# Two turns of a gated linear attention leave TensorE for VectorE blocks and GpSimd transfers

## The chip, the cores and the metric

The kernel runs on one core of one Trainium2 chip. The metric is device time in microseconds (us) of one execution. The kernel before was timed three times: 907.1, 907.38 and 908.11 us, median 907.38 us.

## The reference, cut to what matters

Two layers run one after the other on 256 frames of width 2048. Each layer projects its input once, runs three groups of heads on the result (eight heads of banded softmax attention, four heads of gated linear attention, four heads of cross-attention into 256 memory tokens), gates them, projects back and normalizes. The change touches the linear attention alone:

```python
gate_logit = b_lr @ gate_w + gate_b                 # b_lr: (256, 16), gate_w: (16, 256)
log_g = jax.nn.log_sigmoid(gate_logit) / GATE_TAU
def step(state, inp):                               # one chunk of 64 frames, every head
    qc, kc, vc, gc = inp
    b = jnp.cumsum(gc, axis=1)
    decay = jnp.exp(-jnp.abs(b[:, :, None] - b[:, None, :]))
    attn = jnp.einsum('bihd,bjhd,bijhd->bhij', qc, kc, decay)
    o_intra = jnp.einsum('bhij,bjhv->bihv', attn, vc)
    o_inter = jnp.einsum('bihd,bhdv->bihv', qc * jnp.exp(b), state)
    k_dec = kc * jnp.exp(b[:, -1][:, None] - b)     # decayed keys
    new_state = jnp.exp(b[:, -1])[..., None] * state + jnp.einsum('bjhd,bjhv->bhdv', k_dec, vc)
    return new_state, o_intra + o_inter
```

Two operands stand the wrong way round for TensorE, which sums over partitions. `b_lr` comes out of its projection with frames on partitions, and its product with `gate_w` sums over the 16 gate inputs. `k_dec` is made with features on partitions, and its product with `vc` sums over frames.

## The kernel before, in words

All large projections have one form. A weight piece is loaded by SyncE's queue (SP) into `raw`; ScalarE (ACT) rounds it into a high part `wh` (L124), VectorE (DVE) subtracts to make the low part `wl` (L125), and TensorE multiplies the parts with high and low parts `x` of the input into `acc`. Three products stand for one product in full precision. The pools hold four buffers each of `raw`, `wh` and `wl`, so a cast into `wh` waits until TensorE has finished the piece four before it. A piece is 388 or 512 columns wide.

The order of TensorE's and SP's instructions is that of the program text. Heads are Python generators: after every weight piece of the big projections a clock called `tick` moves on (by 1 for 512 columns, by 0.76 for 388) and the generators that are due put their matrix products between two pieces. A `yield 6` in a generator means that its next products stand at least six ticks later in TensorE's order. Two generators are in turn at a time, three once the linear attention is done. The order on DVE, ACT and GpSimd (POOL) is chosen by the build's scheduler from its own estimate of when things are ready; on the chip each engine then keeps that order, and an instruction that waits holds up everything behind it on its engine.

`gla` is the generator of the linear attention, once per layer. Its steps in the kernel before:

- `lr` holds the 16 gate inputs with frames on partitions, three times side by side (high, low, high; columns 48 to 127 are zero). TensorE turns it with two transposes against an identity (L366), DVE copies the result to `lrT` (L368). `yield 2`.
- Two products of `gw` and `lrT` give the gate's logits (first product at L372, issued through L102), ACT adds the bias (L375), and the chain L378 (DVE), L379 and L380 (ACT, Exp and Ln, each with a table of its own), L381 and L386 (DVE, the last one the cumulative sum `b_`) follows.
- The decayed keys `kd`: a subtraction (L390, DVE), an Exp (L392, ACT) and the product with the keys (L393, DVE). `qe`, `eb` and `elast` are made beside it. `yield 6`.
- TensorE turns `kd` with four transposes (L419) into a PSUM bank; ACT copies it to `kdT` (L421). `yield 2`.
- Twelve small products of `kdT` with the values (`kv` banks), 32 products of undecayed keys and queries, and 32 products of the first level of `decayed` (L404 to L412: subtraction on DVE, Abs and Exp on ACT, two products `kl` and `ql` on DVE). They all stand in one block in TensorE's order. The further levels and the output follow later.

In the trace, scratch tiles, `kd` and `kdT` among them, all carry the name `sc`, and all PSUM banks the name `bk`.

Another way of turning is used elsewhere in the same kernel: `turned` (L549 to L559). DVE turns every 32x32 block of a tile in place of the block (L554), POOL issues one transfer of the tile to a DRAM buffer `home` (L556), waits for its landing, and issues four transfers back, each to 32 partitions, with the blocks in their new places (L559).

Of the kernel before, what the change touches and what calls it, by code (L numbers as in the profile page):

```python
# [8 lines left out]
F32 = mybir.dt.float32  # L9
F32R = mybir.dt.float32r  # L10
# [8 lines left out]
P = 128  # L19
D = 2048  # L20
T = 256
# [15 lines left out]
def hybrid_trunk_kernel(  # L37
# [7 lines left out]
    pe, dve, act, pool, sp = nc.tensor, nc.vector, nc.scalar, nc.gpsimd, nc.sync  # L45
# [30 lines left out]
    def finish(gens):  # L76
        while not all(g in done for g in gens):
            tick()

    def enter(name, bufs=1, **kw):  # L80
        return ctx.enter_context(tc.tile_pool(name=name, bufs=bufs, **kw))
# [5 lines left out]
    hd = enter("hd", 1)  # L87
    tp = enter("tp", 3)
    sc = enter("sc", 8)
    sm = enter("sm", 1)  # L90
    psd = enter("psd", 2, space=bass.MemoryType.PSUM)
    psa = enter("psa", 4, space=bass.MemoryType.PSUM)
    drm = enter("drm", 6, space=bass.MemoryType.DRAM)
# [3 lines left out]
    def nm(s):  # L97
        uid[0] += 1
        return f"{s}_{uid[0]}"

    def mm(o, l, r, start, stop):
        pe.matmul(o, l, r, start=start, stop=stop, skip_group_check=True)  # L102

    def bank():
        return psa.tile([P, 512], F32, name=nm("bk"), tag="bk")

    def scratch(shape, dtype=F32):
        return sc.tile(shape, dtype, name=nm("sc"), tag="sc")
# [4 lines left out]
    ident = cst.tile([P, P], F32, name="ident")  # L113
# [180 lines left out]
    def as_group(src, xq, n, kp=2, first=None, need={}):  # L294

        acc = psd.tile([P, 2, 512], F32, name=nm("acc"), tag="acc")
        for pc in range(16 // kp):
            if first is not None and pc % 2 == 0:
                xq.append(load_quarter(first[pc // 2]))
            finish(need.get(pc, ()))  # L300
            w = piece(src[pc], n, kp)
            for kk in range(kp):
                for t in range(2):
                    as_products(acc[:, t, :n], t, xq, w, pc * kp + kk, kk)
            tick(n / 512)
        return acc
# [12 lines left out]
    def gla_inputs(l):  # L319

        gw = sm.tile([P, 256], F32R, name=nm("gw"), tag="gw")
        raw = hd.tile([48, 256], F32, name=nm("gwraw"), tag="pairs0")
        gb = small([P, 2], "gb")
        ng = small([P, 1], "ng")
        for i in range(3):
            sp.dma_start(raw[i * 16:i * 16 + 16], gate_w[l])
        pool.memset(gw.bitcast(F32), 0.0)
        tc.keep_in_program_order(act.copy(gw[:48], raw))
        tc.keep_in_program_order(dve.tensor_tensor(gw[32:48], raw[32:], gw[32:48].bitcast(F32), op=ALU.subtract))
        sp.dma_start(gb, gate_b[l])  # L330
        sp.dma_start(ng, norm_g[l])
        return gw, gb, ng

    def gla(gw, gb, ng, gq, gk, lr, asv, yraw):
        gqf = gq.rearrange("p b t -> p (b t)")
        gkf = gk.rearrange("p b t -> p (b t)")
        pairs = [hd.tile([P, 4, CH], F32, name=nm("pairs"), tag=f"pairs{par}") for par in range(2)]
# [23 lines left out]
                    dve.copy_predicated(pairs[par], lmask[:, lev].unsqueeze(1).to_broadcast([P, 4, CH]), pv)  # L361


        pt = bank()
        for t in range(2):
            pe.transpose(pt[:, t * P:(t + 1) * P], lr[:, t].bitcast(F32), ident)  # L366
        lrT = sm.tile([P, T], F32R, name=nm("lrT"), tag="lrT")
        dve.tensor_copy(lrT, pt[:, :T])  # L368
        yield 2
        pl = bank()  # L370
        for b in range(2):
            mm(pl[:, b * T:(b + 1) * T], gw[:, b * P:(b + 1) * P], lrT, True, True)  # L372
        xx = scratch([P, 512])
        for b in range(2):
            act.activation(xx[:, b * T:(b + 1) * T], pl[:, b * T:(b + 1) * T], AF.Identity, bias=gb[:, b:b + 1])  # L375
# [13 lines left out]
        kd = scratch([P, 512])  # L389
        dve.tensor_tensor(kd.rearrange("p (g c) -> p g c", c=CH),  # L390
                          bc[:, :, CH - 1:CH].to_broadcast([P, 8, CH]), bc, op=ALU.subtract)
        act.activation(kd, kd, AF.Exp, scale=1.0 / 16)  # L392
        dve.tensor_tensor(kd, gkf, kd, op=ALU.mult)  # L393
        eb = scratch([P, 512])
        act.activation(eb, b_, AF.Exp, scale=1.0 / 16)
        elast = small([P, 8], "elast")
# [16 lines left out]
            return kl, ql  # L413


        pt = bank()
        for t in range(2):
            for b in range(2):
                pe.transpose(pt[:, (t * 2 + b) * P:(t * 2 + b + 1) * P], kd[:, b * T + t * P:b * T + t * P + P], ident)  # L419
        kdT = scratch([P, 4, P])  # L420
        act.copy(kdT, pt.rearrange("p (g c) -> p g c", c=P))  # L421
        yield 2
        nxt = [decayed(LEVELS[0])]
        kv = [bank() for _ in range(2)]
        for c in range(3):
            rs = slice((c % 2) * 64, (c % 2) * 64 + 64)
            t = c // 2
            for b in range(2):
                for par in range(2):
                    h = 2 * b + par  # L430
                    mm(kv[c % 2][par * 64:par * 64 + 64, (t * 2 + b) * P:(t * 2 + b + 1) * P],
                       kdT[rs, t * 2 + b, par * 64:par * 64 + 64],
                       asv[rs, t, 16 + h * P:16 + (h + 1) * P], True, True)

        low, high = bank(), bank()
# [3 lines left out]
        st = hd.tile([P, 3, 2, P], F32, name=nm("st"), tag="st")  # L439
        for c in range(3):  # L440
            t = c // 2
# [29 lines left out]
        for t in range(2):  # L471
            for b in range(2):
                g = t * 2 + b
# [5 lines left out]
        for odd, even in ((1, 2), (3, None)):  # L479
            for b in range(2):  # L480
                for c in (odd, even):
                    if c is not None:
                        for par in range(2):
                            g = (c // 2) * 2 + b
# [64 lines left out]
    def turned(n, *todo):  # L549

        homes = []
        for _, src in todo:
            blocks = scratch([P, 4, n])
            dve.transpose(blocks.rearrange("p b (g j) -> p g b j", j=32), src.rearrange("p (g b j) -> p g b j", b=4, j=32))  # L554
            homes.append(drm.tile([P, 4, n], F32, name=nm("home"), tag=f"home{n}"))
            pool.dma_start(homes[-1], blocks)  # L556
        for (dst, _), home in zip(todo, homes):
            for b in range(4):
                pool.dma_start(dst[b * 32:(b + 1) * 32], home[:, b].rearrange("(a i) n -> i a n", a=4))  # L559
# [72 lines left out]
    def transposed(xq, gbT):  # L632

        raw, gT = gbT
        pt = bank()
        pe.transpose(pt[:, :P], raw, ident)
        dve.tensor_copy(gT, pt[:, :32])
        for q in range(4):
            x = operand()
            hi, lo, _ = x  # L640
            xq.append(x)
            for j in range(0, 4, 2):
                pt = bank()
                y = scratch([P, 2, T])
                for jj in range(2):
                    kt = q * 4 + j + jj
                    for t in range(2):
                        pe.transpose(pt[:, jj * T + t * P:jj * T + (t + 1) * P], res[:, t, kt * P:(kt + 1) * P], ident)  # L648
                with tc.high_priority(AHEAD // 4):
                    for jj in range(2):  # L650
                        kt = q * 4 + j + jj
                        src, g, b = pt[:, jj * T:(jj + 1) * T], gT[:, kt:kt + 1], gT[:, 16 + kt:17 + kt]
                        if jj == 0:
                            act.activation(y[:, jj], src, AF.Identity, bias=b, scale=g)
                        else:
                            dve.tensor_scalar(y[:, jj], src, g, b, op0=ALU.mult, op1=ALU.add)
                    parts(hi[:, j:j + 2], lo[:, j:j + 2], y)
                yield 1

    def restored(gb):  # L660

        for n in range(WO_N):
            for t in range(2):
                r = res[:, t, columns(n)]
                tc.keep_in_program_order(dve.tensor_tensor(r, r, gb[n][0], op=ALU.mult))
                dve.tensor_tensor(r, r, gb[n][1], op=ALU.add)
                yield 2
# [150 lines left out]
    for l in range(L):  # L818
# [20 lines left out]
        else:  # L839
            memq = []  # L840
            parts(*mv, as_group(w512[l, G_MV], memq, 512, 2, memT))
            gens = [transposed(xq, gbT), restored(gb)]
# [5 lines left out]
        gq = hd.tile([P, 2, T], F32, name=nm("gq"), tag="gq")  # L848
        gk = hd.tile([P, 2, T], F32, name=nm("gk"), tag="gk")
# [9 lines left out]
        gp = gla_inputs(l)  # L859
# [6 lines left out]
        asv = per.tile([P, 2, 1552], F32, name=nm("asv"), tag="asv")  # L866

        def values(i):
            acc = as_group(w388[l, i], xq, 388)
            act.copy(asv[:, :, i * 388:(i + 1) * 388], acc[:, :, :388])  # L870
# [9 lines left out]
        lr = hd.tile([P, 2, P], F32R, name=nm("lr"), tag="qe")  # L880
        pool.memset(lr.bitcast(F32), 0.0)
        values(0)
        for i in (0, 32):
            act.copy(lr[:, :, i:i + 16], asv[:, :, :16])
        dve.tensor_tensor(lr[:, :, 16:32], asv[:, :, :16], lr[:, :, :16].bitcast(F32), op=ALU.subtract)
        values(1)
        if l == 0:
            sp.dma_start(res, xn.rearrange("(t p) d -> p t d", p=P))
# [9 lines left out]
            finish(gens)  # L898
        yraw = [per.tile([P, 4, T], F32, name=nm("yr"), tag=f"yr{i}") for i in range(4)]
        finish(early_gens)  # L900
        gens = [[gla(*gp, gq, gk, lr, asv, yraw[0])]]
        waiting.extend(gens[0])
        linear[:] = gens[0]
        for half in range(2):
# [35 lines left out]
        gb = []  # L940
# [148 lines left out]
```

## Time and profile before

| what | value |
|---|---|
| median of three runs | 907.38 us |
| profiled execution, its own time | 907.3 us |
| its span (first to last instruction) | 905.5 us |
| granted TensorE clock, mean | 0.999 |
| TensorE busy (matmul row) | 898.8 us |
| DVE, ACT, POOL busy | 605.4, 480.3, 176.0 us |
| bytes moved by DMA | 207.16 MB |

The views used below are the page's busy line and its chain of work that ended last, the waits of one engine, and the timeline (start and length in us, engine, line, operation, written tile<-read tiles, partitions x elements, count, and in brackets the idle time of the engine just before and what ended it). Times of the timeline count from the span's start. In the timeline, matmuls overlap each other, so what one costs is read from the distance between the starts of its neighbours, not from its own length.

### The profile page before, as it was taken

How to read it: one execution, taken by the hardware profiler on the slowest of the kernel's cores; microseconds unless marked ns; L12 is line 12 of the kernel's file. 1: busy time of each engine (PE TensorE's matmuls, PEld its weight loads, DVE VectorE, ACT ScalarE, POOL GpSimd, SP SyncE). 2: the span in 40 equal slices, each digit the busy share in tenths (PEclk: the TensorE clock that was granted, in tenths of full speed). 3: DMA queues.
4: the chain of work that ended last, by engine and by line, in shares of the span. 5: the costliest groups of instructions: out<-in, count | busy, mean ns of one | idle time of the engine just before them, and what ended most of it. 6: DMA issues, size and time to landing. Idle time of an engine off the chain costs nothing.

```text
span 905.5 us, 13967 instructions
## 1 busy us (share of the span) xinstructions
PE 898.8 (99%) x4926; PEld 773.8 (85%) x4926; DVE 605.4 (67%) x878; ACT 480.3 (53%) x695; POOL 176.0 (19%) x329
## 2 busy tenths in 40 slices
PE   9999999999999999999999999999999999999997
PEld 8889998998888888888888899889888888888885
DVE  6765478757566676565587676885756586766766
ACT  6654475474544656433466445754745365744440
POOL 0002002015043543200000220021141433334000
PEclk9999999999999999999999999999999999999999
DMA  9977876668787988776775686666696879889752
GB/s 313 319 214 216 299 219 194 182 205 268 216 245 206 275 260 274 225 263 188 232 250 168 202 245 204 198 194 202 192 287 195 261 209 277 253 232 280 232 164 93
DMA packets 131512, 207.16 MB, mean 229 GB/s; under 512 B 14313, under 2 KB 99689, under 8 KB 131185
## 3 DMA queue, kind: packets, MB, share of 16 engines
q1 hardware_dynamic: 117744, 173.28, 61.3%
q0 software_dynamic: 13408, 32.59, 13.1%
q8 instruction: 38, 0.62, 0.3%
q10 hardware_dynamic: 288, 0.39, 0.1%
q14 instruction: 34, 0.27, 0.1%
HBM read 189.93 MB, written 16.25 MB: 228 GB/s over the span
## 4 chain that ended last, share of the span: by engine, by line
PE 99%; DMA 0%; DVE 0%; ACT 0%; issue 0%
PE acc L102 90%; PE bk L102 8%; PE bk L648 0%; DMA raw<-w 0%; PE bk L419 0%; ACT res L804 0%; DVE stats L789 0%; PE bk L366 0%; DVE res L788 0%; ACT wh L124 0%; DVE res L740 0%; DVE mvt L743 0%; PE bk L792 0%; ACT nparts L124 0%; DVE rs_u L751 0%
## 5 line engine op out<-in xcount | busy, mean ns | idle before, releaser
L102 PE MATMUL acc<-wh,x 128*128 128x512 f32 (+2 forms) x2196 | 656.2, 380 | 0.2 <-ACT wh L124 0.2
L125 DVE TENSOR_TENSOR wl<-raw,wh 128x1024 fp32r<-128x1024 f32 (+3 forms) x321 | 368.0, 1151 | 190.2 <-ACT wh L124 188.5
L124 ACT CAST wh<-raw 128x1024 fp32r<-128x1024 f32 (+3 forms) x321 | 318.8, 995 | 320.2 <-PE acc L102 256.4
L102 PEld LDWEIGHTS acc<-wh,x 128*128 128x128 f32 x2196 | 405.5, 188 | 63.4 <-ACT wh L124 0.5
L102 PE MATMUL acc<-wl,x 128*128 128x512 f32 (+2 forms) x1098 | 414.7, 378 | 0.0
L102 PEld LDWEIGHTS acc<-wl,x 128*128 128x128 f32 x1098 | 205.9, 188 | 34.0 <-DVE wl L125 0.4
L556 POOL DMA_DIRECT2D home<-sc x58 | 32.5, 561 | 494.3 <-DVE sc L554 483.9
L102 PE MATMUL acc<-x,wh 128*128 128x512 f32 x288 | 91.1, 398 | 0.0
L102 PEld LDWEIGHTS acc<-x,wl 128*128 128x128 f32 x288 | 54.1, 188 | 12.6
L559 POOL DMA_DIRECT2D pT<-home x96 | 52.6, 554 | 41.4 <-DMA home<-sc 26.7
L102 PE MATMUL acc<-x,wl 128*128 128x256 f32 x288 | 56.7, 278 | 0.0
L102 PEld LDWEIGHTS acc<-x,wh 128*128 128x128 f32 x288 | 44.8, 189 | 1.3 <-ACT wh L124 0.2
L559 POOL DMA_DIRECT2D zT<-home x48 | 26.2, 553 | 32.8 <-DMA home<-sc 17.6
L559 POOL DMA_DIRECT2D yr<-home x48 | 26.1, 551 | 16.2 <-DMA home<-sc 7.9
L554 DVE STREAM_TRANSPOSE sc<-sc 128x512 f32<-128x512 f32 (+1 forms) x36 | 22.6, 642 | 1.9 <-ACT sc L931 1.4
L578 ACT ACTIVATE sc<-sc,mx 128x128 f32<-128x128 f32 (+1 forms) x32 | 14.4, 449 | 17.2 <-DVE mx L576 17.2
L538 DVE TENSOR_TENSOR sc<-zT,yr 128x256 f32<-128x256 f32 x24 | 8.9, 415 | 21.3 <-DMA zT<-home 21.3
L408 ACT ACTIVATE sc<-sc 128x512 f32<-128x512 f32 x12 | 7.6, 633 | 14.9 <-DVE sc L406 14.9
L124 ACT CAST x<-sc 128x512 fp32r<-128x512 f32 x20 | 11.8, 617 | 7.0 <-DVE sc L538 5.7
L571 DVE SCALAR_TENSOR_TENSOR sc<-bk,bias 128x384 f32<-128x384 f32 x16 | 8.7, 543 | 9.5 <-PE bk L102 9.5
L554 DVE STREAM_TRANSPOSE sc<-acc 128x512 f32<-128x512 f32 x18 | 11.8, 693 | 3.6 <-PE acc L102 2.8
L559 POOL DMA_DIRECT2D qk<-home x24 | 13.1, 553 | 5.0 <-DMA home<-sc 5.0
(211 smaller groups left out, 587.5 us busy)
## 6 DMA issues: line engine op xcount, KB each, us to landing
raw<-w SPq DMA_DIRECT2D x323, 256.0 KB, 4.2
raw<-w SPq DMA_DIRECT2D x94, 512.0 KB, 4.9
raw<-w SPq DMA_DIRECT2D x64, 388.0 KB, 3.5
home<-sc POOLq DMA_DIRECT2D x42, 256.0 KB, 4.4
bias<-relw SPq DMA_DIRECT2D x16, 192.0 KB, 4.6
yr<-home POOLq DMA_DIRECT2D x48, 64.0 KB, 4.7
home<-sc POOLq DMA_DIRECT2D x16, 192.0 KB, 3.2
pT<-home POOLq DMA_DIRECT2D x64, 48.0 KB, 4.2
```

The lines of the kernel that those rows point to most:

```text
L102: pe.matmul(o, l, r, start=start, stop=stop, skip_group_check=True)
L124: act.copy(hi, src)
L125: dve.tensor_tensor(lo, src, hi.bitcast(F32), op=ALU.subtract)
L408: act.activation(dd, dd, AF.Abs)
L538: dve.tensor_tensor(o, z, r, op=ALU.mult)
L554: dve.transpose(blocks.rearrange("p b (g j) -> p g b j", j=32), src.rearrange("p (g b j) -> p g b j", b=4, j=32))
L556: pool.dma_start(homes[-1], blocks)
L559: pool.dma_start(dst[b * 32:(b + 1) * 32], home[:, b].rearrange("(a i) n -> i a n", a=4))
L571: dve.scalar_tensor_tensor(s, pb[:, :384], SCALE, bias[h], op0=ALU.mult, op1=ALU.add)
L578: act.activation(s[:, own[t]], s[:, own[t]], AF.Exp, bias=mx[:, t:t + 1], accum_out=zs[:, t:t + 1])
```

## The change

Both turns of the linear attention use DVE and POOL. For `lr`, DVE turns 32x32 blocks of its first 64 columns right after `lr` is made, POOL writes them to a DRAM buffer and reads them back with two transfers into a 64-partition `lrT`; the transposes L366, the copy L368 and the `yield 2` behind them are gone, and the gate products read 64 rows of `gw`. For `kd`, the existing `turned` is called right after `kd` is made, into a new tile `kdr`; the four transposes L419 are gone, and ACT's copy into `kdT` reads `kdr` in SBUF and not a PSUM bank.

```diff
-        pt = bank()
-        for t in range(2):
-            pe.transpose(pt[:, t * P:(t + 1) * P], lr[:, t].bitcast(F32), ident)
-        lrT = sm.tile([P, T], F32R, name=nm("lrT"), tag="lrT")
-        dve.tensor_copy(lrT, pt[:, :T])
-        yield 2
         pl = bank()
         for b in range(2):
-            mm(pl[:, b * T:(b + 1) * T], gw[:, b * P:(b + 1) * P], lrT, True, True)
+            mm(pl[:, b * T:(b + 1) * T].rearrange("p (t a j) -> p t a j", t=2, j=32), gw[:64, b * P:(b + 1) * P],
+               lrT.rearrange("p a (t j) -> p t a j", t=2), True, True)
...
         dve.tensor_tensor(kd, gkf, kd, op=ALU.mult)
+        kdr = hd.tile([P, 4, P], F32, name=nm("kdr"), tag="st")
+        turned(P, (kdr, kd))
...
-        pt = bank()
-        for t in range(2):
-            for b in range(2):
-                pe.transpose(pt[:, (t * 2 + b) * P:(t * 2 + b + 1) * P], kd[:, b * T + t * P:b * T + t * P + P], ident)
         kdT = scratch([P, 4, P])
-        act.copy(kdT, pt.rearrange("p (g c) -> p g c", c=P))
+        act.copy(kdT.rearrange("p g (a j) -> p g a j", j=32), kdr.rearrange("p a (g j) -> p g a j", j=32))
         yield 2
...
-                       kdT[rs, t * 2 + b, par * 64:par * 64 + 64],
+                       kdT[rs, b * 2 + t, par * 64:par * 64 + 64],
...
         dve.tensor_tensor(lr[:, :, 16:32], asv[:, :, :16], lr[:, :, :16].bitcast(F32), op=ALU.subtract)
+        lrT = sm.tile([64, 4, 64], F32R, name=nm("lrT"), tag="lrT")
+        blocks = scratch([P, 2, 64])
+        dve.transpose(blocks.rearrange("p b (t j) -> p t b j", j=32), lr[:, :, :64].bitcast(F32).rearrange("p t (b j) -> p t b j", j=32))
+        home = drm.tile([P, 2, 64], F32, name=nm("home"), tag="home64")
+        pool.dma_start(home, blocks)
+        for b in range(2):
+            pool.dma_start(lrT[b * 32:(b + 1) * 32].bitcast(F32), home[:, b].rearrange("(a i) n -> i a n", a=4))
```

TensorE's order in the first layer, at the block that uses the turned keys. `acc` is the accumulator of the projection for the first four softmax heads, whose third piece (`wh_1249` before, `wh_1262` after) ends here; `sc_1125` is `kd`, `sc_1272` and `sc_1240` are `kdT`. Before, the third piece ends, the transposes stand, and two more pieces follow until the block:

```order
L102 MATMUL acc_1209<-wl_1250,x_371 128x512
L419 MATMUL bk_1267<-ident,sc_1125 128x128 x4
L102 MATMUL acc_1209<-wh_1275,x_371 128x512 x2
L102 MATMUL acc_1209<-wl_1276,x_371 128x512
```

```order
L102 MATMUL acc_1209<-wl_1295,x_448 128x512
L102 MATMUL bk_1320<-asv_718,sc_1272 64x128 x4
L102 MATMUL bk_1321<-asv_718,sc_1272 64x128 x4
L102 MATMUL bk_1320<-asv_718,sc_1272 64x128 x4
L102 MATMUL bk_1334<-gq_530,gk_531 64x64
```

After the change the block stands behind the third piece itself (the `64x64` products of `sc_1285` and `sc_1284` are the first level of `decayed`, 32 in all):

```order
L102 MATMUL acc_1220<-wl_1263,x_371 128x512
L102 MATMUL bk_1288<-asv_718,sc_1240 64x128 x4
L102 MATMUL bk_1289<-asv_718,sc_1240 64x128 x4
L102 MATMUL bk_1288<-asv_718,sc_1240 64x128 x4
L102 MATMUL bk_1302<-gq_530,gk_531 64x64
```

The block has moved ahead of two pieces, to the place where the four transposes stood. In the same way the gate products now stand where the two transposes of `lr` stood, one piece behind the start of the projection `acc_1036`.

ACT's order in the first layer after the change, from the table load for Exp to the next weight casts (`sc_1073` is `kd` in the making, `sc_1086` is `eb`, `sc_1280` the first level of `decayed`):

```order
L387 ACT_TABLE_LOAD
L387 ACTIVATE sc_1073<-sc_1073 128x512
L124 COPY wh_1222<-raw_1221 128x1024
L392 ACTIVATE sc_1086<-b_1068 128x512
...
L124 COPY wh_1392<-raw_1391 128x1024
L414 COPY sc_1240<-kdr_1077 128x512
L405 ACTIVATE sc_1280<-sc_1280 128x512
L406 ACTIVATE sc_1280<-sc_1280 128x512
L124 COPY wh_1411<-raw_1410 128x1024
```

The Exp of `kd` has moved ahead of that of `eb`, and the copy into `kdT`, which now waits for a transfer, stands ahead of the Abs and Exp of the first level.

POOL's order in the first layer after the change:

```order
L552 DMA qk_532<-home_692 32x4x128 x4
L883 DMA home_877<-sc_875 128x128
L885 DMA lrT_874<-home_877 32x4x64 x2
L327 MEMSET gw_4908 128x256
L379 MEMSET sc_1069 128x512
L380 MEMSET sc_1069 128x8
L549 DMA home_1080<-sc_1078 128x512
L552 DMA kdr_1077<-home_1080 32x4x128 x4
L549 DMA home_1469<-sc_1467 128x512
```

The transfers of `lr` are new between the turn of the projected queries and keys (`qk_532`) and the three memsets, and those of `kd` (`home_1080`, `kdr_1077`) between the memsets and the next turn. The second layer has the same rows in the same places.

More of the change, by code (lines that the diff above doesn't have):

```diff
@@ L332, in gla_inputs, with gla @@
         return gw, gb, ng
-    def gla(gw, gb, ng, gq, gk, lr, asv, yraw):
+    def gla(gw, gb, ng, gq, gk, lrT, asv, yraw):
         gqf = gq.rearrange("p b t -> p (b t)")
@@ L900, in hybrid_trunk_kernel @@
         finish(early_gens)
-        gens = [[gla(*gp, gq, gk, lr, asv, yraw[0])]]
+        gens = [[gla(*gp, gq, gk, lrT, asv, yraw[0])]]
         waiting.extend(gens[0])
```

## The prediction

> **What bounds the kernel now.** I read the page's busy line first, then its chain of work that ended last, then the waits of TensorE alone, and last the timeline around the two turns in both layers.
>
> ```profile
> PE 898.8 (99%) x4926; PEld 773.8 (85%) x4926; DVE 605.4 (67%) x878; ACT 480.3 (53%) x695; POOL 176.0 (19%) x329
> PE 99%; DMA 0%; DVE 0%; ACT 0%; issue 0%
> ```
>
> ```profile
> PE bk L102 <- DVE eps L817: 1.1, 1, 1.1
> ...
> PE acc L102 <- ACT wh L124: 0.2, 1, 0.2
> ```
>
> TensorE is the chain from end to end, and the view of its waits has four rows (first and last shown; each one wait, none longer than 1.1 us), none of them in `gla`. So two things alone can move the time: TensorE work that goes, and waits that come. DVE and POOL have room; what they add costs nothing unless TensorE waits for it.
>
> **What goes.** The transposes stand between projections whose pace is even, so their cost is read from the starts of their neighbours.
>
> ```profile
> 107.01 0.34 PE L102 MATMUL acc<-wl,x 128*128 128x388 f32 x1
> ...
> 107.54 0.34 PE L102 MATMUL acc<-wl,x 128*128 128x388 f32 x1
> 107.72 0.38 PE L366 MATMUL bk<-ident,lr 128*128 128x128 f32 x2
> ...
> 108.28 0.34 PE L102 MATMUL acc<-wl,x 128*128 128x388 f32 x1
> ```
>
> ```profile
> 130.25 0.39 PE L102 MATMUL acc<-wl,x 128*128 128x512 f32 x1
> ...
> 130.93 0.39 PE L102 MATMUL acc<-wl,x 128*128 128x512 f32 x1
> 131.16 0.60 PE L419 MATMUL bk<-ident,sc 128*128 128x128 f32 x4
> ...
> 132.07 0.40 PE L102 MATMUL acc<-wl,x 128*128 128x512 f32 x1
> ```
>
> From one `wl` product to the next it is 107.54 - 107.01 = 0.53 us, and 108.28 - 107.54 = 0.74 us where the two transposes of `lr` stand: 0.21 us. Likewise 130.93 - 130.25 = 0.68 us and 132.07 - 130.93 = 1.14 us: 0.46 us for the four of `kd`. Per layer 0.67 us, for two layers **-1.34 us**. The gate products keep their 256 columns and lose only idle rows, so I leave their cost as it was; a change of pace by the new access pattern is bounded by their pair's 0.40 us either way per layer (row below), and I take nothing. DVE's copy L368 goes too, which nobody waits for now.
>
> **What comes: a turn that must land in time.** The gate products move to the place of the two transposes, and the block of small products to the place of the four. So the distance from one to the other is about the same as between the two transposes, but a journey through DRAM now lies in it. I follow it step by step.
>
> ```profile
> 110.06 0.84 ACT L124 CAST wh<-raw 128x776 fp32r<-128x776 f32 x1 [1.48 <-PE acc L102]
> 115.05 0.83 ACT L375 ACTIVATE sc<-bk,gb 128x256 f32<-128x256 f32 x2
> 117.61 0.62 ACT L379 ACTIVATE sc<-sc 128x512 f32<-128x512 f32 x1
> 118.25 1.28 ACT L380 ACT_TABLE_LOAD   x1
> ```
>
> ```profile
> 115.18 0.97 DVE L125 TENSOR_TENSOR wl<-raw,wh 128x776 fp32r<-128x776 f32 x1 [1.15 <-ACT wh L124]
> 116.06 0.68 DVE L378 SCALAR_TENSOR_TENSOR sc<-sc 128x512 f32<-128x512 f32 x1
> 121.00 1.23 DVE L386 TENSOR_TENSOR_SCAN b<-sc,sc 128x512 f32<-128x512 f32 x1
> 125.67 0.68 DVE L393 TENSOR_TENSOR sc<-gk,sc 128x512 f32<-128x512 f32 x1
> ```
>
> ```profile
> 114.28 0.40 PE L102 MATMUL bk<-lrT,gw 128*128 128x256 f32 x2
> ```
>
> First layer, durations from these rows, in the order that the changed program has. Gate products 107.72 to 108.1. ACT is in a cast until 108.6, bias to 109.4, DVE's L378 to 110.1. ACT: the cast at 110.06, which waits for its buffer, to 110.9, Exp to 111.5, table to 112.8, Ln (as long as Exp) to 113.4. DVE: L381 (as L378) to 114.1, one subtraction to 115.1, sum to 116.3, L390 (as long as L393) to 117.0. ACT: Exp to 117.7 (its table is loaded by then). DVE: one subtraction to 118.0, the product `kd` to 118.7. Then the new part: block transpose 0.65, and 0.36 us until POOL issues (rows below): **home issued at 119.7**.
>
> ```profile
> 554.05 0.38 PE L366 MATMUL bk<-ident,lr 128*128 128x128 f32 x2
> ...
> 577.55 0.60 PE L419 MATMUL bk<-ident,sc 128*128 128x128 f32 x4
> ```
>
> ```profile
> 556.41 0.84 ACT L124 CAST wh<-raw 128x776 fp32r<-128x776 f32 x1 [1.50 <-PE acc L102]
> ```
>
> Second layer: the same, but ACT's order has a table load before the first Exp too, and TensorE's places are those of the two rows above. From 554.05: bias to 555.7, cast to 557.25, load, Exp, load, Ln to 561.1; DVE's L381 to 561.8. Two casts and the third load hold ACT until 564.1; DVE's subtraction to 562.9, sum to 564.1, L390 to 564.8; Exp to 565.4, product behind a subtraction to 566.5: **home issued at 567.5**.
>
> Length of a turn, from POOL's issue to the start of the reader:
>
> ```profile
> 71.88 1.31 DVE L554 STREAM_TRANSPOSE sc<-acc 128x512 f32<-128x512 f32 x2 [1.10 <-PE acc L102]
> ...
> 81.72 0.29 DVE L854 COPY gk<-qk 128x256 f32<-128x256 f32 x1 [1.82 <-DMA qk<-home]
> ```
>
> ```profile
> 72.90 1.27 POOL L556 DMA_DIRECT2D home<-sc  x2 [71.61 <-DVE sc L554]
> 75.65 4.37 POOL L559 DMA_DIRECT2D qk<-home  x8 [1.48 <-DMA home<-sc]
> ```
>
> ```profile
> 519.22 1.16 POOL L556 DMA_DIRECT2D home<-sc  x2 [14.73 <-DVE sc L554]
> ```
>
> ```profile
> 528.47 0.29 DVE L854 COPY gk<-qk 128x256 f32<-128x256 f32 x1 [2.23 <-DMA qk<-home]
> ```
>
> Both readers stood waiting for the transfer, so these are true lengths: 81.72 - 72.90 = 8.8 us and 528.47 - 519.22 = 9.25 us, for a tile of the same shape. I take 9.0 us.
>
> [...]
>
> What stands behind the landing: ACT's copy, then, queued behind it on ACT, the Abs and Exp of the first level, then DVE's `kl` and `ql`, which the block's last 32 products need.
>
> ```profile
> 132.08 0.58 ACT L421 COPY sc<-bk 128x512 f32<-128x512 f32 x1
> ```
>
> ```profile
> 134.50 0.69 DVE L412 TENSOR_TENSOR sc<-gq,sc 128x512 f32<-128x512 f32 x1
> ```
>
> ```profile
> 137.18 0.97 PE L102 MATMUL bk<-asv,sc 64*64 64x128 f32 x21
> ...
> 138.51 0.22 PE L102 MATMUL bk<-sc,sc 64*64 64x64 f32 x1
> ```
>
> From the copy's start to `ql` it is 135.19 - 132.08 = 3.1 us. The block begins at 131.16 - 0.21 = 130.95 and asks for `ql` 138.51 - 137.18 = 1.33 us later, at 132.3; in the second layer at 577.55 - 0.21 + 1.33 = 578.7. First layer: 119.7 + 9.0 + 3.1 = 131.8, so 0.5 us early, **no wait**. Second: 567.5 + 9.0 + 3.1 = 579.6, **a wait of 0.9 us**. A wait comes from 9.5 us of turn on in the first layer and from 8.1 us on in the second.
>
> ```profile
> 90.55 0.19 DVE L885 TENSOR_TENSOR lr<-asv,lr 128x32 fp32r<-128x32 f32 x1
> ```
>
> ```profile
> 146.52 0.68 DVE L412 TENSOR_TENSOR sc<-gq,sc 128x512 f32<-128x512 f32 x1
> ```
>
> ```profile
> 155.87 1.63 PE L102 MATMUL bk<-sc,sc 64*64 64x64 f32 x96
> ```
>
> Three covers hide the rest. `lr` is ready at 90.7 in the first layer and its products stand at 107.7, so its turn has 16 us. ACT's copy stood 5 us ahead of the block (132.08 against 137.18) and now ends just ahead of it, so the levels behind it come up to 5 us later against their products; the last of the three levels used at 155.87 was ready at 147.2, which covers that. And the weight casts queued behind ACT's waiting copy feed pieces that TensorE reaches only after the block and two more pieces (four times 0.68 us each), over 5 us later. Where a cover is gone, each us too late is a us of the end.
>
> **Sum.** 907.3 - 1.34 + 0 + 0.9 = **906.9 us** for the profiled execution, which stands 0.1 us below the median of the runs.
>
> **Rivals.**
>
> *No wait at all.* If the scheduled chain runs 1 us faster than I add up, or the turn lands in 8 us, only the saving is left: 907.3 - 1.34 = 906.0. For it: the overlaps of neighbouring rows (0.1 us each), which I mostly left out. Against: both measured turns are over 8.1 us.
>
> *Long turns (slower).* The store to `home` does not always land as fast:
>
> ```profile
> 214.46 2.17 POOL L559 DMA_DIRECT2D pT<-home  x4 [4.54 <-DMA home<-sc]
> ```
>
> This row's first read came 5.1 us after its store was issued: 4.54 us of idle time that ended with the store's landing, behind the 0.56 us of the issue. At 72.90 it was 2.75 us. A turn with that store takes 8.8 + 2.35 = 11.1 us: waits of 1.6 and 3.0 us, and 907.3 - 1.34 + 4.6 = 910.6. Halfway, at 10.2 us, it is 0.7 + 2.1 - 1.34 = +1.5, 908.8. It turns the sign from 9.5 us of turn on.
>
> [...]
>
> *The gate's turn is late.* At 91 us the largest load of the kernel is in flight:
>
> ```profile
> res<-xn SPq DMA_DIRECT2D x1, 2048.0 KB, 9.2
> ```
>
> If both journeys of `lr` take 9.2 us behind it, the products wait: 91.8 + 9.2 + 0.6 + 9.2 = 110.8 against 107.7, 3.1 us, in the first layer alone: 910.0. Against: `lr`'s transfers are small (64 KB and twice 32 KB).
>
> **How the numbers follow.** Forecast (no wait, then 0.9 us) 0.45; no wait at all 0.17; long turns 0.28; late gate turn 0.10. A measurement of this kernel can tell about 0.2% (1.8 us) from no change. The forecast lies within that; of the first rival 0.05 could come out past it, if the transposes cost more than their neighbours' starts show; of the second about half (0.15) lies above 909.1, of the third 0.08. So faster 0.05, same 0.72, slower 0.23. The range runs from 905.7, just below no wait at all, to 910.0, which leaves out the upper end of the long turns.
>
> **What would show it.** TensorE's row should lose twelve transposes, and its waits gain one line in `gla`: `bk` waiting for DVE's `sc` (first level late) of about 1 us, in the second layer alone. The store of `kd` should be issued near 119.7 and 567, and the copy into `kdT` start 9 us later. If TensorE waits for ACT's copy itself, the turn took over 10 us. If it waits at the gate products, the third rival holds; if a wait stands anywhere else, I have missed a step.

## The result, and the profile after

The kernel after takes 918.75 us (median of six runs, 915.4 to 923.99), the kernel before 907.33 us beside it (six runs, 907.02 to 908.64). The ratio is 1.0123 with a 95% interval of 1.0102 to 1.0144: slower by 1.2%, and 8.75 us above the upper end of the predicted range. The profiled execution took 918.05 us (span 916.3 us, mean granted clock 0.993, against 905.5 us and 0.999).

The busy line of the page and its chain of work that ended last, after:

```profile
PE 903.3 (99%) x4914; PEld 776.2 (85%) x4914; DVE 608.6 (66%) x880; ACT 480.0 (52%) x695; POOL 185.0 (20%) x345
PE 72%; issue 20%; DMA 5%; POOL 2%; DVE 1%; ACT 1%; POOLq 0%; DVEq 0%; ACTq 0%
```

TensorE has lost the twelve transposes (4926 to 4914), yet it is busy for 4.5 us more, and DMA and POOL now stand in the chain ("issue" is time for which the profile shows no wait). The waits of TensorE, after (total, times, longest):

```profile
PE bk L102 <- ACT sc L414: 4.5, 2, 2.4
PE bk L102 <- DVE sc L409: 1.5, 2, 1.0
```

Both rows are new; the four others of this view stand as before. L414 is ACT's copy into `kdT`, L409 is `ql` of the first level; each is waited for once per layer. The journey of `kd` in the timelines of POOL and ACT, after (store, first read, copy, in both layers):

```profile
120.06 0.56 POOL L549 DMA_DIRECT2D home<-sc  x1 [10.55 <-DVE sc L547]
124.36 2.18 POOL L552 DMA_DIRECT2D kdr<-home  x4 [3.75 <-DMA home<-sc]
...
573.60 0.56 POOL L549 DMA_DIRECT2D home<-sc  x1 [23.12 <-DVE sc L547]
577.23 2.17 POOL L552 DMA_DIRECT2D kdr<-home  x4 [3.06 <-DMA home<-sc]
```

```profile
133.02 0.62 ACT L414 COPY sc<-kdr 128x512 f32<-128x512 f32 x1 [5.59 <-DMA kdr<-home]
...
585.52 0.62 ACT L414 COPY sc<-kdr 128x512 f32<-128x512 f32 x1 [5.16 <-DMA kdr<-home]
```

From the store's issue to the copy it is 133.02 - 120.06 = 13.0 us and 585.52 - 573.60 = 11.9 us. The bracket on each copy says that ACT stood idle for it. The prediction had said that a wait for the copy itself would mean a turn of over 10 us; it does. TensorE's timeline at the block, first layer and then second, after:

```profile
131.26 0.39 PE L102 MATMUL acc<-wl,x 128*128 128x512 f32 x1
133.69 0.97 PE L102 MATMUL bk<-asv,sc 64*64 64x128 f32 x21 [2.04 <-ACT sc L414]
...
136.21 1.13 PE L102 MATMUL bk<-sc,sc 64*64 64x64 f32 x32 [0.57 <-DVE sc L409]
137.28 1.22 PE L102 MATMUL acc<-wh,x 128*128 128x512 f32 x2
138.29 0.63 PE L102 MATMUL acc<-wl,x 128*128 128x512 f32 x1
...
139.57 0.63 PE L102 MATMUL acc<-wl,x 128*128 128x512 f32 x1
...
142.06 0.62 PE L102 MATMUL acc<-wh,x 128*128 128x512 f32 x2
```

```profile
583.39 0.39 PE L102 MATMUL acc<-wl,x 128*128 128x512 f32 x1
586.19 0.97 PE L102 MATMUL bk<-asv,sc 64*64 64x128 f32 x21 [2.41 <-ACT sc L414]
...
588.72 1.14 PE L102 MATMUL bk<-sc,sc 64*64 64x64 f32 x32 [0.97 <-DVE sc L409]
589.78 1.22 PE L102 MATMUL acc<-wh,x 128*128 128x512 f32 x2
...
592.30 0.63 PE L102 MATMUL acc<-wh,x 128*128 128x512 f32 x2
```

Before, the block that starts at 137.18 came 0.31 us behind the last `wl` product:

```profile
136.87 0.39 PE L102 MATMUL acc<-wl,x 128*128 128x512 f32 x1
```

So it was due at 131.57 and 583.70, and came 2.1 and 2.5 us late. The products of `ql` were due 1.33 us into the block and came 2.52 and 2.53 us into it, 1.2 us late in each layer. Together 7.0 us of waiting.

Behind the block something else stands out: 138.29 to 139.57 is 1.28 us from one `wl` product to the next, where 0.68 us is this kernel's pace. The windows show why (length, busy time of PE, PEld, DVE, ACT and POOL, granted clock, DMA share, GB/s), first layer and then second:

```profile
134.00:134.50 0.50, 0.50 (x24) 0.50 (x18) 0.00 (x0) 0.47 (x2) 0.00 (x0) 1.00 0.02 8
135.00:141.00 6.00, 5.42 (x63) 4.34 (x60) 6.00 (x10) 2.97 (x4) 0.00 (x0) 0.50 0.28 96
141.50:142.00 0.50, 0.50 (x3) 0.42 (x3) 0.50 (x3) 0.47 (x1) 0.00 (x0) 1.00 0.82 262
...
588.00:588.50 0.50, 0.00 (x0) 0.00 (x0) 0.50 (x2) 0.50 (x2) 0.00 (x0) 1.00 0.16 33
589.00:592.00 3.00, 3.00 (x37) 2.48 (x34) 3.00 (x5) 1.47 (x3) 0.00 (x0) 0.50 0.17 30
```

The clock was granted at half for close to 7 us in the first layer and for about 3.5 us in the second. In the first layer it fell about 1 us into the block, after the wait of 2.04 us and ahead of that for `ql`; in the second it fell only around the second wait, the one of 0.97 us. The idle time at the block comes in parts: 2.04 and 0.57 us in the first layer, 2.41 and 0.97 us in the second, with the small products between.

Its price is read from the same products before and after. Before, the last 32 products of the block and what follows them run so:

```profile
139.13 0.73 PE L102 MATMUL acc<-wh,x 128*128 128x512 f32 x2
...
140.63 0.61 PE L102 MATMUL acc<-wh,x 128*128 128x512 f32 x2
...
141.99 0.39 PE L102 MATMUL acc<-wh,x 128*128 128x512 f32 x1
```

The `ql` products took 139.13 - 138.51 = 0.62 us, four steps of the piece behind them 2.86 us, two steps 1.50. After, in the first layer, 1.07 us and 142.06 - 137.28 = 4.78 us for four: 2.4 us lost. In the second 1.06 us and 592.30 - 589.78 = 2.52 us for two: 1.5 us lost. Together 3.8 us.

Last, the gate products. TensorE's timeline around them, after, and around their old place, before:

```profile
107.14 0.34 PE L102 MATMUL acc<-wl,x 128*128 128x388 f32 x1
...
107.67 0.34 PE L102 MATMUL acc<-wl,x 128*128 128x388 f32 x1
107.93 0.50 PE L102 MATMUL bk<-lrT,gw 64*128 64x256 f32 x2
...
108.83 0.33 PE L102 MATMUL acc<-wl,x 128*128 128x388 f32 x1
```

```profile
114.10 0.34 PE L102 MATMUL acc<-wl,x 128*128 128x388 f32 x1
...
114.86 0.34 PE L102 MATMUL acc<-wl,x 128*128 128x388 f32 x1
```

The pair adds 1.16 - 0.53 = 0.63 us after, and added 0.76 - 0.53 = 0.23 us before: 0.4 us more per layer, which is more than the 0.21 us of the two transposes that it saves.

Sum for the profiled execution, in us: transposes -1.34, gate pairs +0.8, waits +7.0, clock +3.8. That is +10.3; the execution is 10.75 longer. Set side by side, the projections' products of the two traces show the rest as steps of +0.13 us by the first layer's gate and +0.4 us near 383 us, whose cause stays open.

### The profile page after: what moved, and what is told of

The parts are those of the page before. It is cut to its first block, busy times and chain, and to the rows that moved or that the text cites. A ratio compares the mean times of both kernels' runs of the same rounds, so it can differ in the third digit from the quotient of the medians.

```text
span 916.3 us, 13979 instructions
## 1 busy us (share of the span) xinstructions
PE 903.3 (99%) x4914; PEld 776.2 (85%) x4914; DVE 608.6 (66%) x880; ACT 480.0 (52%) x695; POOL 185.0 (20%) x345
## 4 chain that ended last, share of the span: by engine, by line
PE 72%; issue 20%; DMA 5%; POOL 2%; DVE 1%; ACT 1%; POOLq 0%; DVEq 0%; ACTq 0%
PE acc L102 64%; PE bk L102 7%; DMA home<-sc 2%; DMA kdr<-home 1%; DMA raw<-w 1%; DMA qk<-home 0%; DMA zT<-home 0%; POOL qk L552 0%; POOL zT L552 0%; POOL kdr L552 0%; DVE sc L409 0%; DVE wl L125 0%; ACT sc L406 0%; ACT sc L405 0%; POOL lrT L885 0%
## 5 line engine op out<-in xcount | busy, mean ns | idle before, releaser
L552 POOL DMA_DIRECT2D pT<-home x96 | 52.7, 555 | 46.4 <-DMA home<-sc 30.6
L552 POOL DMA_DIRECT2D zT<-home x48 | 26.3, 556 | 32.8 <-DMA home<-sc 14.6
L552 POOL DMA_DIRECT2D yr<-home x48 | 26.1, 551 | 21.0 <-issue 10.4
L408 DVE TENSOR_TENSOR sc<-gk,sc 128x512 f32<-128x512 f32 x12 | 8.3, 690 | 12.4 <-ACT sc L406 12.4
```

What stands on the lines that cost most here:

```text
L408: dve.tensor_tensor(kl, gkf, dd, op=ALU.mult)
```

## The experiments

Each ratio is against runs of the kernel before on the same chip beside it; in brackets its 95% interval. The theory: a turn of 12 to 13 us, made long by weight loads, costs the waits, the waits cost the clock, and 64-row products cost the gate pair. The rivals are with each run.

**One part alone.** The change has two parts that share nothing but the chain between them. In `lr_only`, `kd` is turned by TensorE as before:

```diff
-        kdr = hd.tile([P, 4, P], F32, name=nm("kdr"), tag="st")
-        turned(P, (kdr, kd))
...
+        for t in range(2):
+            for b in range(2):
+                pe.transpose(pt[:, (t * 2 + b) * P:(t * 2 + b + 1) * P], kd[:, b * T + t * P:b * T + t * P + P], ident)
```

> The gate inputs are turned as in the changed kernel, the decayed keys by TensorE as before; the block of small products stands two pieces behind the transposes again. Theory (the journey of the decayed keys and what its wait does to the clock is the whole loss): two times two transposes are saved, 0.43 us, and nothing waits in the linear attention, so 906.5 to 907.5 us, clock 0.999. Rival (the gate's turn, its transfers among the 2 MB load at 91 us, or the shift of everything behind it by two ticks costs): TensorE waits for weights near 104 us or elsewhere, and it is slower by 1 us or more, 908.5 or above.

Measured 908.79 us, 1.0009 [1.0000, 1.0017]: this part costs between nothing and 1.5 us, and saves nothing, so the theory's range (906.5 to 907.5) was missed. The traces set side by side step by +0.41 us at the new pair's place and -0.22 us at the old one's, in the first layer and again in the second. The number is one that the rival allowed (908.5 or above), but TensorE waits for no weights; one wait came that neither had, at the last head over the memory tokens:

```profile
351.50 0.74 PE L102 MATMUL bk<-sc,mv 128*128 128x256 f32 x4 [0.76 <-DVE sc L125]
```

In `kd_only`, `lr` is turned by TensorE and `kd` by DVE and POOL.

> The decayed keys are turned as in the changed kernel, the gate inputs by TensorE as before. Between the gate products and the block there are eight ticks here as there. Theory: the whole loss is here, two waits of TensorE of 3 to 4 us each for ACT's copy and for the first level, followed by a granted clock of about half for several us, 915 to 924 us in all. Rival (the gate's turn has a share): at most half the loss, 910 to 913 us.

Measured 922.12 us, 1.0154 [1.0141, 1.0167], more than the whole change. Its waits of TensorE (its copy is at L419):

```profile
PE bk L102 <- ACT sc L419: 9.0, 2, 5.6
```

So the loss lies with `kd`, apart from the 0.2 us net per layer of the gate products. It is larger than in the whole change because the store is issued later against the block: with the gate's two ticks back, the store goes out at 127.86 us, 8.9 us ahead of the block's due time (the last `wl` product at 136.49 and 0.31 us), where the whole change has 11.5 us; the copy starts at 139.53, a journey of 11.7 us. The clock was 0.67 at 140 to 145 us and 0.50 at 595 to 600 us.

**Why the turn is long.** First the transfers without anybody who waits for them: `turn_beside` is the kernel before with `turned(P, (kdr, kd))` added and its result unused.

> The kernel before with the journey of the decayed keys added and nobody reading what arrives; TensorE's transposes stay. It measures the journey and its price without a wait. Theory: the transfers alone cost nothing, 907.0 to 908.0 us, clock 0.999, and the reads land in 4 to 6 us. Rival (the added transfers push the weight loads back far enough to stop TensorE): waits for wh or wl behind 118 us and 909 us or more.

Measured 908.25 us, 0.9995 [0.9983, 1.0008]: POOL's and DVE's share and the traffic itself cost nothing that the whole time shows. Its first read was issued 5.1 and 5.4 us behind the store, the last one 1.6 us later, and the reads landed 4.1 to 5.9 us after their issue. So the last of them landed at least 10.8 and 11.1 us behind the issue of the store: the turn is long also where nobody waits for it. Then the turn with less beside it: `light` is the kernel after, and loads half of each weight piece of the projection in whose time `kd` travels.

```diff
+                for i, part in enumerate(src[:1] if light[0] else src):
...
+            light[0] = g == G_AQ0
             acc = as_group(halves(g), x, 512)
+            light[0] = False
```

> The changed kernel with half the weights of the first softmax heads' queries left out: each of these pieces loads 256 of its 512 columns and casts them twice, so the traffic of SyncE's queue halves while the decayed keys travel (the result of these heads is not the reference's). Theory (the journey takes 12 to 13 us and not the 9 us of the same shape elsewhere because its reads stand in line with these weight loads): the reads land in 3 to 4.5 us instead of 5.0 to 7.0, the journey takes 9 to 10 us, TensorE waits under 1.5 us per layer, the clock stays at 0.998 or above, 906.5 to 909 us. Rival (the length belongs to the journey itself or to DVE and GpSimd work beside it): journeys of 12 us or more and 915 us or more as before.

Measured 909.99 us, 1.0018 [1.0008, 1.0029]. The journey in POOL's and ACT's timeline of `light` (its lines stand five later):

```profile
119.87 0.56 POOL L554 DMA_DIRECT2D home<-sc  x1 [10.54 <-DVE sc L552]
```

```profile
128.05 0.62 ACT L419 COPY sc<-kdr 128x512 f32<-128x512 f32 x1 [1.16 <-DMA kdr<-home]
...
578.43 0.62 ACT L419 COPY sc<-kdr 128x512 f32<-128x512 f32 x1 [3.43 <-DMA kdr<-home]
```

The journeys are 128.05 - 119.87 = 8.2 us and 578.43 - 569.39 = 9.0 us, TensorE does not wait for the copy, and of the change's 1.23% only 0.18% are left. Half of the weight traffic, with the same work on the engines, makes the difference of 4.8 and 2.9 us. The other runs bear it out: in the seven kernels whose copy waits for `kd` under the full weight loads (the kernel after, `kd_only`, `late_block`, `filler`, `kd_late`, `late128`, `gate128`) the fourteen turns took 11.0 to 13.7 us. The last two columns of the windows give the DMA engines' share and what they moved. `light`, both layers:

```profile
119.90:128.00 8.10, 8.10 (x42) 7.27 (x41) 6.63 (x8) 4.39 (x5) 2.71 (x5) 1.00 0.74 205
569.40:578.40 9.00, 9.00 (x44) 7.78 (x43) 6.71 (x8) 4.31 (x5) 2.73 (x5) 1.00 0.84 212
```

The turns of queries and keys from which I took 9.0 us, before:

```profile
72.90:81.70 8.80, 8.80 (x51) 8.80 (x51) 4.58 (x6) 3.38 (x4) 5.64 (x10) 1.00 0.85 267
519.20:528.50 9.30, 9.30 (x55) 9.30 (x54) 5.76 (x9) 3.43 (x5) 6.12 (x12) 1.00 0.87 242
```

And `kd`, after:

```profile
120.00:133.00 13.00, 11.65 (x56) 9.88 (x54) 6.87 (x8) 4.46 (x5) 2.74 (x5) 1.00 0.90 273
573.60:585.50 11.90, 10.18 (x48) 8.42 (x46) 6.72 (x8) 4.31 (x5) 2.74 (x5) 1.00 0.94 285
```

Here the turns of 12 and 13 us have the highest shares. That is no threshold: the second turn of `kd_only` took 12.6 us at a mean share of 0.84. What is shown is that fewer loads beside the turn shorten it; which queue or memory makes it wait is not.

Both legs are shorter in `light`. Its first read was issued 2.6 us behind the store in both layers (122.50 - 119.87 and 572.02 - 569.39), where the kernel after has 4.3 and 3.6 us, and its reads landed 3.5 to 4.9 us after their issue, where the kernel after has 5.0 to 7.0.

What `light` keeps is the gate pair, 0.6 us of waiting for `ql` in the second layer, and 1.6 us at the same memory head as in `lr_only`.

**Wait and clock apart.** `late_block` is the kernel after with the block two ticks later, which puts two weight pieces ahead of it:

```diff
-        yield 6
+        yield 8
```

> The changed kernel with a yield of 8 in place of 6 ahead of the block, which puts it two weight pieces (5.4 us) later in TensorE's order. Theory (only the time that the journey has decides): the waits of 2.6 and 1.2 us per layer are gone, the clock stays at 0.999, and only the saving of twelve transposes is left: 905.7 to 906.7 us, below both kernels. Rival (the later levels and heads run into waits of their own, or ACT's copy holds up the weight casts behind it): waits of TensorE for wh or wl behind the block, 908 us or more.

Measured 910.53 us, 1.0036 [1.0024, 1.0048], clock 0.999. Both waits at the block and the half clock are gone, and the ratio falls from 1.0123 to 1.0036, but not below 1, as the theory had it. Two new waits are the rival's kind: 1.4 us at the memory head, and 0.7 us for `wl` near 599 us, whose casts stand in ACT's order behind the Exp of a further level.

`filler` keeps the block in its place and fills the wait: sixteen products of 512 columns into an unused bank stand ahead of it.

```diff
+        junk = bank()
+        for _ in range(16):
+            mm(junk, xq[0][0][:, 0, :P], xq[0][2][:, 0], True, True)
         kv = [bank() for _ in range(2)]
```

> The changed kernel with 16 products of 512 columns ahead of the block whose result nobody reads (3.6 us per layer, as long as TensorE waits there now). They do nothing for the result, they only keep TensorE at work. Theory (idle time makes the granted clock fall to about half for 7 us behind the wait, and that is half of the loss): the clock stays at 0.999 and the time falls by 4 to 6 us though TensorE has 7 us more to do, 912 to 914.5 us. Rival (the clock falls for another reason, or the waits alone are the loss): same time as the changed kernel, 916 to 920 us, or slower by the filler.

Measured 916.44 us, 1.0096 [1.0083, 1.0109]. TensorE's timeline and windows of `filler`:

```profile
131.03 3.79 PE L102 MATMUL bk<-x 128*128 128x512 f32 x16
134.74 0.97 PE L102 MATMUL bk<-asv,sc 64*64 64x128 f32 x21
```

```profile
134.00:138.00 4.00, 4.00 (x98) 3.32 (x97) 3.98 (x6) 3.13 (x4) 0.00 (x0) 1.00 0.01 4
...
588.00:592.00 4.00, 4.00 (x33) 3.28 (x24) 4.00 (x6) 1.28 (x3) 0.00 (x0) 1.00 0.40 131
```

The block starts 134.74 - 131.03 = 3.71 us behind the fillers' start, later than in the kernel after (133.69), and the clock stays at 1.00. With 7.4 us more work on TensorE the kernel takes no longer than the kernel after, and rather less (0.96% over the kernel before against 1.23%, though the two intervals still touch). That shows the clock to be the idle time's doing and a loss of its own. The saving is less than expected, and the traces size it better than the times: side by side with the kernel before, the stretch of the first layer's block grows by 3.16 us here and by 5.23 after, that of the second by 3.58 and 4.67; so 2.1 and 1.1 us are the clock's net share, and a wait of 0.5 us at the memory head and 0.7 us for `wl` came on top.

**The gate pair.** Two things are new on it: 64 rows instead of 128, and a strided pattern of its operand and output. `rows64` is the kernel before with 64 rows and nothing else.

```diff
-            mm(pl[:, b * T:(b + 1) * T], gw[:, b * P:(b + 1) * P], lrT, True, True)
+            mm(pl[:, b * T:(b + 1) * T], gw[:64, b * P:(b + 1) * P], lrT[:64], True, True)
```

> The kernel before, whose gate products read 64 rows in place of 128, and nothing else. Theory (a product of 64 rows between products of 128 costs the pair 0.4 us): 0.8 us slower, 908.3 to 909.0 us beside 907.8 of before. Rival (the runs of 32 in the access pattern cost it): no difference.

Measured 908.76 us, 1.0001 [0.9991, 1.0011]: two pairs are too small for the whole time to tell. The trace tells: side by side with the kernel before, it steps by +0.39 us at the first pair and +0.39 us at the second (and by 0.9 us at the memory head, where TensorE waits again). `gate128` is the kernel after with all 128 columns of `lr` sent on the journey, so the pattern stays and the rows are 128 again.

> The changed kernel, but the gate products read 128 rows again (all 128 columns of the gate inputs travel, the last 64 rows are zeros). In the traces with 64 rows the projection around the gate products loses about 0.6 us where the pair of 128 rows lost 0.23. Theory (the change of the array's row count between neighbours costs about 0.4 us per pair): the pair's own row goes from 0.50 back to about 0.40 us and the projection behind it starts 0.3 to 0.4 us earlier. Rival (the access pattern in runs of 32 costs it): unchanged, 0.50 and 0.6 us. The whole time can't tell in one look: 915 to 922 us either way.

One execution, 917.3 us. TensorE's timeline of `gate128`:

```profile
108.30 0.34 PE L102 MATMUL acc<-wl,x 128*128 128x388 f32 x1
108.48 0.40 PE L102 MATMUL bk<-lrT,gw 128*128 128x256 f32 x2
...
109.07 0.34 PE L102 MATMUL acc<-wl,x 128*128 128x388 f32 x1
```

109.07 - 108.30 = 0.77 us, so the pair costs 0.24 us, as before the change (0.23). The rows did it, and the pattern costs nothing; why 64 rows cost more is not shown. The block's waits remained (5.9 us for the copy in two waits).

**How much there was to win.** `no_turn` is the kernel before without either turn; the products read what has not been turned.

> The kernel before without either turn: TensorE's twelve transposes and DVE's copy are left out, the gate products read the unturned inputs, and ACT copies the unturned keys (the result is not the reference's). The order of everything else stays. It is the most that the change could have won. Theory of the prediction: the whole saving reaches the end, 1.34 us, 906.3 to 906.9 us beside 907.8 of before. Rival (the last memory head of the first layer, whose probabilities arrive at 350.0 us just when TensorE asks for them in the kernel before, takes back what the first layer saves): half of it, 0.5 to 0.8 us, with a wait of TensorE near 350 us that before does not have.

Measured 907.13 us, 0.9986 [0.9977, 0.9995], that is -1.3 us [-2.1, -0.5]. Side by side the traces step by -0.22, -0.43, -0.26 and -0.52 us at the four places, -1.43 together. That is the most that any way of turning elsewhere can win in this order, and there was no wait at the memory head.

**A better version.** `kd_late` is `kd_only` with `yield 8`; `late128` is the kernel after with `yield 8` and 128 rows at the gate.

> The decayed keys alone are turned by VectorE and GpSimd, and the block stands two pieces later (yield 8 in place of 6); the gate inputs stay with TensorE. Theory: without the gate's pair of 64 rows (0.2 us lost per layer) and with the journey hidden only the eight transposes are saved, 0.96 us; the kernel with the late block lost 1.9 us in a wait of the last memory heads near 351 us and 0.9 us near 599 us, which belong to the order that came with it. If these come here too: 907.5 to 909.5 us; if not: 906.0 to 907.0 us. Rival (a journey under TensorE's work still stops it at the block): waits for ACT's copy and 910 us or more.

Measured 912.73 us, 1.0057 [1.0043, 1.0071], above both of the theory's ranges. The number is one that the rival allowed (910 or more), but not for its reason: the block no longer waits for the copy. Instead the accumulators of projections wait for DVE's next block transposes (L552 there), beside 1.4 us at the memory head:

```profile
PE acc L102 <- DVE sc L552: 1.4, 2, 1.1
```

> The changed kernel with the block two pieces later and with gate products of 128 rows. Theory: the late block's 910.5 us less 0.8 us of the pairs, 909.2 to 910.2 us, no wait at the block, clock 0.999. It would beat the kernel before only if the waits near 351 and 599 us went too. Rival (the rest of the late block's loss is the block itself): 911 us or more.

Measured 908.73 us, 1.0006 [0.9997, 1.0015]: the least loss of the versions that take `kd` off TensorE, and no better than the kernel before. Its turn still takes 12.2 us (119.43 to 131.66), hidden now. Nothing waits at the block or at the memory head. What takes the saving back are late weight casts, above all in the second layer, where TensorE's products fall behind by 1.9 us near 597 us (in the first by 0.9 us near 169 us). ACT's and TensorE's rows there:

```profile
594.54 0.63 ACT L405 ACTIVATE sc<-sc 128x512 f32<-128x512 f32 x1 [3.74 <-DVE sc L403]
```

```profile
598.36 0.50 PE L102 MATMUL acc<-x,wl 128*128 128x256 f32 x2 [0.79 <-DVE wl L125]
```

It is not the copy that holds these casts up, which ended 13 us ahead of the first row: they stand in ACT's order behind the Abs and Exp of the fourth level, for which ACT waits 3.7 us. In the kernel before, ACT starts that step at 590.04 us.

## Why the prediction was wrong, step by step

**What goes: right.** -1.34 us predicted; `no_turn` measured -1.3 us, its trace -1.43.

**The way to the store: right.** Issue at 119.7 us predicted, 120.06 measured. In the second layer 567.5 is moved by what the first layer had lost (5.2 us at the block, 0.2 at the gate pair, 0.1 and 0.4 elsewhere) to 573.4; 573.60 measured. From the copy to `ql`, 3.1 us predicted, and DVE's L409, from 135.47 to 136.16, says the same (136.16 - 133.02 = 3.1).

**Length of a turn: wrong, and the step that decided.** "I take 9.0 us": it was 13.0 and 11.9. The shape of the tile was the same as in the two turns that I measured, the neighbours were not, and I did not ask which loads would be in flight with it; `light` shows that this traffic makes the difference. The old kernel's traffic in these stretches would not have told: the changed kernel moved 273 and 285 GB/s there, the one before 178 and 166.

What the old trace did show is that the two turns taken were short ones. Their stores landed after 2.3 to 2.7 us; the view of its transfers gives, as medians over the whole kernel, for the stores of 256 KB and for the largest group of reads:

```profile
home<-sc POOLq DMA_DIRECT2D x42, 256.0 KB, 4.4
yr<-home POOLq DMA_DIRECT2D x48, 64.0 KB, 4.7
```

With three issues of 0.55 us between the first read and the last this is 10.8 us, an estimate, and by the prediction's own formula waits of 1.3 and 2.7 us, which puts the sum at 910.0, the upper end of the range.

My rival of long turns named the right step. Its late store was enough (5.1 us from the store's issue to the first read, where 4.3 and 3.6 were measured), but it left the reads as they were; they took 5.0 to 7.0 us to land, and that made up most of the rest. With 0.28 for such turns I still let the range end inside their span.

**The waits' formula: right.** A wait from 9.5 us of turn on in the first layer and from 8.1 in the second gives, with 13.0 and 11.9 us, 3.5 + 3.8 = 7.3 us; 7.0 were measured. With the true turn the sum would have been 907.3 - 1.34 + 7.3 = 913.3.

**The clock: missing.** I priced each us too late as a us of the end. It cost 3.8 us more, since TensorE slowed to half behind the wait; `filler` and `late_block`, with a mean clock of 0.998 and 0.999, show that it stays up where the idle time is filled or gone. The kernel before has no wait in this stretch, so its trace could not show this. What length of idling it takes is not shown.

**The gate products: wrong in size.** "I leave their cost as it was": each pair cost 0.4 us more, +0.8 in all. The bound that I named, 0.40 us per layer, was just reached, but I looked for a cause in the access pattern, and `gate128` and `rows64` show that it was the 64 rows.

**The gate's turn: right.** It was not late, though slow: its store alone took 7.2 us to the first read (91.58 to 98.77), and the reads landed at most 5.6 us after their issue, about 3 us ahead of the products at 107.9.

**Left open.** The wait at the last memory head is 0 to 1.6 us in these kernels. In the kernel before, DVE's part of that head ends at 349.99 us and its product starts at 350.00: no margin. Why some orders push it over and others (`gate128`, `late128`, `no_turn`) don't was not settled.

## What to carry to other kernels

The length of a transfer is to be taken from a transfer in the same traffic, not from one of the same shape: the same tile took 13.0 and 11.9 us beside the full weight loads and 8.2 and 9.0 us beside half of them. Where the margin is a fraction of a us, the step is priced with the longest that the trace has for both its legs. The waits on TensorE cost more than their length here, 3.8 us of clock on top of 7.0 us of waiting, so such a wait is either left out (`late_block`) or filled (`filler`). TensorE waited for 1.9 us in all in the kernel before, and what was to be saved was 0.15% of the time: the change, which puts a journey through DRAM in the path, could win 1.3 us at most (`no_turn`), and lost 11.

## What the runs showed of the hardware

- Clock: in the kernel after, TensorE's granted clock fell from 1.00 to 0.50 about 1 us behind an idle time of 2.04 us in the first layer, and in the second layer, where one of 2.41 us came before the block, only at a further 0.97 us of idling within it. It was back after close to 7 and about 3.5 us. A single wait of 1.4 us (`late_block`) left the mean at 0.999.
- Rows: a pair of products with 64 rows between products with 128 rows took 0.63 us of TensorE's time, the same pair with 128 rows 0.23 to 0.24 us.
- Transfers: the turn of a 256 KB tile by way of DRAM, one store and four reads, took 11.0 to 13.7 us under this kernel's full weight loads and 8.2 and 9.0 us with half of them (`light`).
